# Start of a hybrid mLSTM / S5 / gated-FFN layer: S5 parameters loaded earlier and worked on between the statistics of x, the condition spread by PE transposes, the normalisation bias made on POOL

## The chip, the core and the metric

One core of one Trainium2 chip runs the kernel. The metric is the time of one execution on the device in microseconds (us); the kernel before has a median of 870.68 us over 3 runs (870.36 to 873.5).

## The reference, cut to what matters

One layer over x (512 tokens of 1024 features) with a condition vector c of 1024. Everything is float32.

```python
c_act = silu(c)
sh1, sc1, g1, sh2, sc2, g2 = split(c_act @ w_ada + b_ada, 6)
h   = standardize(x) * (1 + sc1) + sh1            # 512 x 1024
proj = h @ w_in + b_in                            # parts: mLSTM input, gates, S5 input, mixing gates
# S5 part, per state: dt = exp(log_dt); mag = exp(lam_re*dt); ar + i*ai = mag*(cos, sin)(lam_im*dt)
#   (zr, zi) from ar, ai, lam; powers of the rotation; a scan over the tokens
# mLSTM part: conv, q, k, v, chunked gated attention, norm, down projection
x = layer_norm(ALPHA * x + (1 + g1) * mix)        # then a gated FFN of 2816 and a second layer norm
```

## The kernel before, in words

**Layout.** Tokens lie in four tiles of 128 (`xt`), features in eight blocks of 128 (j or k = 0 to 7). A float32 product is made of three float32r matmuls (`mm3`, lines 255 to 258): high part by high part, high by low, low by high. So every operand is split first: ACT writes the high part (line 231) and DVE subtracts to get the low part (line 234).

**Start.** SP issues all loads from one queue, in program order: the small columns `cols`, the condition c broadcast over all 128 partitions (`CA`, 128 x 1024), the identity, the four x tiles, then the first weights (`wa1`, `w0`), then `lam`, the S5 parameters. ACT and DVE turn `CA` into c*(1+tanh(c/2)) in two halves (lines 308 to 311). A small copy `ca` (128 x 8, c with feature on partition) is made from `cols` at lines 312 to 316. For each x tile DVE takes statistics (`stats`: two of line 302, one of line 303), POOL makes the reciprocal deviation `rs` (lines 295, 296), DVE makes the bias `nb` = -mean*rs (line 329), and ACT normalises (line 324). While this runs, PE is kept busy with 34 matmuls on zeros (`warm`, line 338), and 9 more after the last transposes of the first block.

**Block steps k0 to k7 (`kstep`).** Step j needs scale and shift of feature block j: `ada1` (lines 343 to 348) multiplies two 128 x 1024 weight tiles by `CA` on DVE with a running sum, one per column of scale and shift. `htr(j)` transposes block j of the four normalised x tiles on PE (line 355), ACT applies scale and shift (line 357), and the result is split into `hp[j]`. Then PE runs 6 x 3 matmuls of 512 columns into six accumulators. Within step j the work for block j+1 is issued: its loads, `ada1(j+1)`, its weight split, and, after two of the six products, `htr(j+1)`.

**S5 parameters.** `s5_scalars` (lines 402 to 505) is a generator. Up to its first `yield` it works on DVE on 128 x 16 tiles: `exp_acc` (14 short instructions) for dt, a second `exp_acc` for mag, and polynomials for sine and cosine. The two stages after it are some 85 short POOL instructions (line 372 and its neighbours): `a1`, `zc` and the powers, then `epow` and the tables `e8`. `s5_params(q)` builds from them, for each of four groups q: `AB` (DVE, needs `zc` and the powers), its PE transposes into `G` (line 543), `TT`, `F` (DVE), and `E` (DVE, needs `e8`; line 208).

**What orders the work.** `SEQ` is an order written out by hand: each `S` advances the S5 generator to its next `yield`, each `H` the head generator (gates first, then four mLSTM heads), `u`, `x`, `o`, `g` are projection tiles. A planner then fills every engine's queue in that order of priority: an instruction of lower priority is put in where it reckons that the higher ones are not ready yet. `keep` fixes the order of some instructions of one engine, and `tc.issue_after(i)` puts a block's instructions behind instruction i on i's engine. At run time each engine works its queue in order, so an instruction that waits holds up all behind it on that engine.

The first gate work on PE are eight line 669 and four line 674 matmuls, then DVE computes the forget gates (lines 676 to 691), POOL lays them out (lines 698, 699) and PE transposes them (line 705).

Of the kernel before, what the change touches and what calls it, by code (L numbers as in the profile page):

```python
# [16 lines left out]
P = 128  # L17
# [37 lines left out]
def pack(i):  # L55
    f = np.float32
    a = {k: np.asarray(v) for k, v in i.items()}
    o = {}
    o["x"] = a["x"][0]
    wa = a["w_ada"][0].reshape(KD, P, 6, KD, P)  # L60
    o["wa1"] = wa[:, :, [1, 0]].transpose(3, 4, 2, 0, 1).reshape(KD, P, 2 * D)
    o["c"] = a["c"].reshape(1, D)
    o["wa2"] = wa[:, :, [4, 3, 2, 5]].reshape(KD, P, 4 * D)
    perm = np.arange(S).reshape(4, KD, C5).transpose(0, 2, 1).reshape(-1)
    w_in = a["w_in"][0]
    b_in = a["b_in"][0]
    o_i = 2 * D
    o_us = o_i + 8
    o_ga = o_us + S
    gg = np.arange(2 * D).reshape(2, KD, P).transpose(1, 0, 2).reshape(-1) + o_ga  # L70
    order = np.concatenate([o_us + perm, np.arange(o_i), gg])
    wt = w_in[:, order].reshape(KD, P, 36, P)
    bmain = b_in[order]
    o["w0"] = wt[:, :, :NXM0].reshape(KD, P, NXM0 * P)
    o["win"] = wt[:, :, NXM0:].transpose(2, 1, 0, 3).reshape(36 - NXM0, P, D)
    wg = np.zeros((KD, P, 32), f)
    wg[:, :, :8] = w_in[:, o_i:o_us].reshape(KD, P, 8)
    o["wg"] = wg.transpose(1, 0, 2).reshape(P, KD * 32)
    wq = a["w_mlstm_q"][0].reshape(2, 2, 2, P, QK)
    wk = a["w_mlstm_k"][0].reshape(2, 2, 2, P, QK)  # L80
    o["wqk"] = np.stack([wq, wk], 2).transpose(0, 4, 1, 2, 3, 5).reshape(2, P, D)
    o["wdn"] = a["w_mlstm_down"][0].reshape(KD, P, KD, P).transpose(2, 1, 0, 3).reshape(KD, P, D)
    o["wglu"] = a["w_s5_glu"][0][perm].reshape(4, P, 2, KD, P).transpose(3, 1, 2, 0, 4).reshape(KD, P, D)
    o["wmix"] = a["w_mix_out"][0].reshape(KD, P, D)
    o["wup"] = a["w_ffn_up"][0].reshape(KD, P, 2, NF, P).transpose(3, 2, 1, 0, 4).reshape(2 * NF, P, D)
    o["wfd"] = a["w_ffn_down"][0].reshape(NF, P, D)
    cols = np.zeros((P, NCOLS), f)

    def put(name, v):
        s, n = COLS[name]  # L90
        cols[:, s:s + n] = v

    ada = a["b_ada"][0].reshape(6, KD, P)
    put("c", a["c"][0].reshape(KD, P).T)
    put("ada1", ada[[1, 0]].transpose(2, 0, 1).reshape(P, 16))
    put("ada2", ada[[4, 3]].transpose(2, 0, 1).reshape(P, 16))
    put("b_in", bmain.reshape(36, P).T)
    put("b_gate", np.broadcast_to(b_in[o_i:o_us], (P, 8)))
    put("cw", a["w_mlstm_conv"][0].reshape(4, KD, P).transpose(2, 0, 1).reshape(P, 32))
    put("cb", a["b_mlstm_conv"][0].reshape(KD, P).T)  # L100
    put("gain", a["mlstm_norm_gain"][0].reshape(KD, P).T)
    put("d", a["s5_d"][0][perm].reshape(4, P).T)
    put("fw", a["w_ffn_conv"][0].reshape(3, NF, P).transpose(2, 0, 1).reshape(P, 66))
    put("fb", a["b_ffn_conv"][0].reshape(NF, P).T)
    o["rows"] = np.stack([ada[2].reshape(-1), ada[5].reshape(-1), a["ln1_gain"][0], a["ln1_bias"][0],
                          a["ln2_gain"][0], a["ln2_bias"][0]])
    lam = np.zeros((P, 3, NG), f)
    lam[:, 0] = a["s5_lam_re"][0].reshape(NG, P).T
    lam[:, 1] = a["s5_lam_im"][0].reshape(NG, P).T
    lam[:, 2] = np.repeat(a["s5_log_dt"][0].reshape(NG, 2).T, N5, 0)  # L110
    o["lam"] = lam.reshape(P, 3 * NG)
    bc = np.stack([np.stack([a["s5_b_re"][0], a["s5_b_im"][0]]),
                   np.stack([a["s5_c_re"][0], a["s5_c_im"][0]]).transpose(0, 1, 3, 2)])
    o["s5bc"] = bc.reshape(2, 2, 4, 4, P, C5).transpose(4, 2, 0, 1, 3, 5).reshape(P, 4, 256)
    o["ident"] = np.eye(P, dtype=f)
    mk = np.zeros((P, 16), f)
    mk[np.arange(16), np.arange(16)] = 1.0
    mk[32 + np.arange(16), np.arange(16)] = 1.0
    put("mask", mk)
    sg = np.zeros((P, 8), f)  # L120
    for j in range(8):
        sg[j::32, j] = 1.0
    put("selg", sg)
    o["cols"] = cols
    sh = np.zeros((P, T5, P), f)
    for t in range(T5):
        for s in range(t + 1):
            for q in range(C5):
                sh[(t - s) * C5 + q, t, (T5 - 1 - s) * C5 + q] = 1.0
    o["shift"] = sh.reshape(P, T5 * P)  # L130
    return {k: np.ascontiguousarray(v) for k, v in o.items()}
# [11 lines left out]
QUICK = (1, 3)  # L143
LAST = ((0, 0, 512), (1, 0, 256), (1, 256, 512))
SEQ = """
k0 S k1 S k2 k3 k4 S S S k5 k6 S S k7 H u0 x3 S S x2 S u1 u2 x1 S x0 H H o0 o3 S S S H H H H S S S H o1 S x5 H
H u3 H H H H S x6 o2 H H o4 H x7 S H H S H S H H H o6 S H H S x4 S S H H S o7 o5 H S H H S H g10 H H H H S g00
S S H S S S H H H S g20 H S H S S g01 H H H H H g30 H H H g11 S g31 S H H H H g21 A l0 A H H A g70 S l2 d0 S S
l1 d1 d2 g40 A g50 l3 A g41 A g51 S A A H H d3 l4 g60 R g61 A A A A A A l5 A A A d4 A A A l6 A A A d5 g71 l7
# [10 lines left out]
def _build(ctx, tc, nc, h):  # L160
# [9 lines left out]
    def const(shape, dt=F32):  # L170
        uid[0] += 1
        return sb.tile(list(shape), dt, name="k_%d" % uid[0])

    def bank(tag):
        return tl(tag, [P, 512], pool=ps)
# [7 lines left out]
    def hx(n=512, dt=F32, parts=P, tag="hx"):  # L183
        return tl(tag, [P, 516], dt)[:parts, :n]

    def hh(n=512, dt=F32, parts=P):
        return hx(n, dt, parts, "hh")
# [4 lines left out]
    def dma(o, i):  # L192
        return nc.sync.dma_start(o, i)  # L193

    def ts(o, i, a, b=None, op0=ALU.mult, op1=None):
        if op1 is None:
            V.tensor_scalar(o, i, a, None, op0=op0)
        else:
            V.tensor_scalar(o, i, a, b, op0=op0, op1=op1)

    def stt(o, i0, s, i1, op0=ALU.mult, op1=ALU.add, acc=None):
        if acc is None:
            V.scalar_tensor_tensor(o, i0, s, i1, op0=op0, op1=op1)  # L203
        else:
            V.scalar_tensor_tensor(o, i0, s, i1, op0=op0, op1=op1, accum_out=acc)

    def tt(o, a, b, op=ALU.mult):
        V.tensor_tensor(o, a, b, op=op)  # L208
# [14 lines left out]
    def keep(i):  # L223
        e = i.ins.engine
        if e in kept:
            tc.add_manual_dep(i.ins, kept[e].name, mybir.DependencyInfo(mybir.DependencyClass.NoSync, mybir.DependencyReason.DATA),
                              reason="order")
        kept[e] = i.ins

    def split_into(hi, lo, x, pin=False):  # L230
        i = A.copy(hi, x)  # L231
        if pin:
            keep(i)
        i = V.tensor_tensor(lo, x, f32(hi), op=ALU.subtract)  # L234
        if pin:
            keep(i)

    def wsplit(ap, n=D, tags=("wh", "wl"), w=None, pin=False):
        w = wload(ap, n) if w is None else w
# [21 lines left out]
    dma(cols, h["cols"])  # L261
    XB = const([P, 2, 4, 2, K5])
    CA = XB.rearrange("p r a g k -> p (r a g k)")
    dma(CA, h["c"].to_broadcast([P, D]))
    ident = const([P, P])
    dma(ident, h["ident"])
    xt = []
    for t in range(NT):
        xt.append(wload(h["x"][t * P:(t + 1) * P, :], tag="gab"))
# [6 lines left out]

    was = wa_load(0)
    w0 = w0_load(0)
    lam = const([P, 3, NG])
    dma(lam.rearrange("p a b -> p (a b)"), h["lam"])  # L280
    wgt = hx(256)
    dma(wgt, h["wg"])

# [21 lines left out]
        rstd_of(rs, mv[:, 1:2], 1)  # L305
        return mv[:, 0:1], rs

    for i, tw in enumerate((hx(), hh())):
        c_ = CA[:, i * 512:(i + 1) * 512]
        keep(A.activation(tw, c_, AF.Tanh, scale=0.5))  # L310
        stt(c_, tw, 1.0, c_, ALU.add, ALU.mult)
    th = const([P, 8])
    A.activation(th, col("c", 0, 8), AF.Tanh, scale=0.5)
    ca = const([P, 8])
    stt(ca, th, 1.0, col("c", 0, 8), ALU.add, ALU.mult)
    ts(ca, ca, 0.5)
    bhalf = const([P, 36])
    ts(bhalf, col("b_in", 0, 36), 0.5)
    norm = []
# [6 lines left out]
    for t, x in enumerate(xt):  # L326
        mu, rs = stats([x[:, :512], x[:, 512:]])
        nb = tl("nb", [P, 1], bufs=4)
        keep(V.scalar_tensor_tensor(nb, mu, -1.0, rs, op0=ALU.mult, op1=ALU.mult))
        norm.append((nb, rs))  # L330
        x_norm(t, 0, D if t < 2 else P)

# [10 lines left out]
    def ada1(j, wa):  # L343
        r = tl("adr", [P, 2], bufs=2)
        for i in range(2):
            keep(V.scalar_tensor_tensor(wa[i], wa[i], 0.5, CA, op0=ALU.mult, op1=ALU.mult, accum_out=r[:, i:i + 1]))
        keep(V.scalar_tensor_tensor(sc1[:, j:j + 1], r[:, 0:1], 1.0, col("ada1", j), op0=ALU.add, op1=ALU.add))
        keep(V.tensor_tensor(sh1[:, j:j + 1], r[:, 1:2], col("ada1", 8 + j), op=ALU.add))

# [52 lines left out]
    def s5_scalars():  # L402
# [23 lines left out]
        exp_acc(dt, lam[:, 2, :], NG)  # L426
        mag, ang = pt16(), pt16()
        tt(t16[0], lr, dt)
        exp_acc(mag, t16[0], NG)
        tt(ang, li, dt)  # L430
        kk = pt16()
        ts(kk, ang, 1.0 / (2 * math.pi), BIG, ALU.mult, ALU.add)
        ts(kk, kk, -BIG, None, ALU.add)
# [310 lines left out]
    acc0 = [acc() for _ in range(2)] + [bank("hd") for _ in range(4)]  # L744
    wbank = acc0[0]
    warm(wbank, 34)
    ada1(0, was)
    w0s = wsplit(None, NXM0 * P, w=w0, pin=True)
    lasttr = htr(0)
    with tc.issue_after(lasttr.ins):  # L750
        warm(wbank, 9)
    for t in (2, 3):
        x_norm(t, P, D)
    w0p = [w0s]
# [532 lines left out]
```

## Time and profile before

| | |
|---|---|
| median of 3 runs | 870.68 us |
| the profiled execution's own time | 870.72 us |
| its span, first to last instruction | 869.0 us |
| mean granted TensorE clock | 0.986 |
| PE busy | 831.4 us, 96% |
| DVE busy | 625.2 us, 72% |
| ACT busy | 366.9 us, 42% |
| POOL busy | 106.3 us, 12% |

The span is the time on the cores' engines; the execution's own time has 1.7 us more around it. A busy time counts instructions in work, not how well they use the engine; matmuls on zeros count as busy too. "Idle before <-" in a row is the time for which the engine stood still before that instruction and what ended the wait. The granted clock is given as a share of full speed (1.00 is 2.4 GHz, 0.50 is 1.2 GHz).

### The profile page before, as it was taken

How to read it: one execution, taken by the hardware profiler on the slowest of the kernel's cores; microseconds unless marked ns; L12 is line 12 of the kernel's file. 1: busy time of each engine (PE TensorE's matmuls, PEld its weight loads, DVE VectorE, ACT ScalarE, POOL GpSimd, SP SyncE). 2: the span in 40 equal slices, each digit the busy share in tenths (PEclk: the TensorE clock that was granted, in tenths of full speed). 3: DMA queues.
4: the chain of work that ended last, by engine and by line, in shares of the span. 5: the costliest groups of instructions: out<-in, count | busy, mean ns of one | idle time of the engine just before them, and what ended most of it. 6: DMA issues, size and time to landing. Idle time of an engine off the chain costs nothing.

```text
span 869.0 us, 11151 instructions
## 1 busy us (share of the span) xinstructions
PE 831.4 (96%) x4005; PEld 669.6 (77%) x4005; DVE 625.2 (72%) x1169; ACT 366.9 (42%) x585; POOL 106.3 (12%) x256
## 2 busy tenths in 40 slices
PE   6979999999999999999999999999999999999996
PEld 2756778787778778888887988888888878888885
DVE  5967888978779785558988858566666675878144
ACT  3445445553565533223334456444444444334000
POOL 2298121112022000000002200000000000000000
PEclk8889999999999999999999999999999999999999
DMA  8742231222222243558656013224344232445011
GB/s 318 256 150 89 67 106 37 83 70 85 66 63 65 72 137 129 186 186 285 227 172 216 14 49 121 97 93 139 135 142 146 98 121 73 157 160 172 22 49 48
DMA packets 45558, 106.45 MB, mean 122 GB/s; under 512 B 13376, under 2 KB 14272, under 8 KB 45504
## 3 DMA queue, kind: packets, MB, share of 16 engines
q1 hardware_dynamic: 45504, 105.75, 36.8%
q8 instruction: 31, 0.51, 0.2%
q14 instruction: 23, 0.19, 0.1%
HBM read 101.54 MB, written 2.10 MB: 119 GB/s over the span
## 4 chain that ended last, share of the span: by engine, by line
PE 68%; DVE 15%; POOL 6%; ACT 4%; DMA 3%; issue 2%; SPq 2%; DVEq 0%; ACTq 0%; POOLq 0%
PE acc L258 10%; PE acc L257 10%; PE hd L256 10%; PE acc L256 10%; PE hd L258 10%; PE hd L257 10%; POOL k L372 3%; DVE hh L203 2%; DVE wl L234 2%; SPq L193 2%; DVE s5h L208 2%; PE s L256 1%; PE s L257 1%; PE s L258 1%; PE s L636 1%
## 5 line engine op out<-in xcount | busy, mean ns | idle before, releaser
L231 ACT CAST wh<-w 128x1024 fp32r<-128x1024 f32 (+2 forms) x103 | 103.1, 1003 | 143.4 <-PE acc L257 107.4
L234 DVE TENSOR_TENSOR wl<-w,wh 128x1024 fp32r<-128x1024 f32 (+2 forms) x103 | 120.9, 1175 | 57.8 <-ACT wh L231 56.0
L256 PE MATMUL acc<-hp,wh 128*128 128x512 f32 x256 | 103.0, 407 | 4.8 <-ACT hp L231 4.2
L257 PE MATMUL acc<-hp,wh 128*128 128x512 f32 x256 | 102.0, 399 | 0.3 <-DVE hp L234 0.3
L258 PE MATMUL acc<-hp,wl 128*128 128x512 f32 x256 | 101.8, 398 | 0.0
L256 PE MATMUL hd<-s5b,wh 128*128 128x512 f32 (+1 forms) x168 | 63.2, 379 | 0.7 <-ACT s5b L1199 0.5
L257 PE MATMUL hd<-s5b,wh 128*128 128x512 f32 (+1 forms) x168 | 63.7, 380 | 0.1
L258 PE MATMUL hd<-s5b,wl 128*128 128x512 f32 (+1 forms) x168 | 63.5, 379 | 0.0
L256 PEld LDWEIGHTS acc<-hp,wh 128*128 128x128 f32 x256 | 48.7, 192 | 18.3 <-ACT hp L231 6.3
L203 DVE SCALAR_TENSOR_TENSOR hh<-hh,hh 128x512 f32<-128x512 f32 x52 | 36.0, 692 | 31.2 <-ACT hh L591 14.7
L257 PEld LDWEIGHTS acc<-hp,wh 128*128 128x128 f32 x256 | 48.9, 191 | 10.1 <-DVE hp L234 1.0
L258 PEld LDWEIGHTS acc<-hp,wl 128*128 128x128 f32 x256 | 48.9, 191 | 9.8
L203 DVE SCALAR_TENSOR_TENSOR s5h<-hh,k,s5h 128x512 f32<-128x512 f32 x56 | 39.3, 747 | 3.3 <-DMA hh<-in_wa 3.0
L1054 POOL TENSOR_SCALAR mov<-mov 128x1 f32<-128x1 f32 x6 | 4.3, 724 | 274.5 <-ACT s L1053 158.5
L256 PEld LDWEIGHTS hd<-s5b,wh 128*128 128x128 f32 x168 | 31.3, 188 | 7.6 <-ACT s5b L1199 0.8
L257 PEld LDWEIGHTS hd<-s5b,wh 128*128 128x128 f32 x168 | 31.6, 188 | 7.2 <-DVE s5b L234 0.6
L258 PEld LDWEIGHTS hd<-s5b,wl 128*128 128x128 f32 x168 | 31.6, 188 | 6.4
L203 DVE SCALAR_TENSOR_TENSOR hh<-hh,k,hh 128x512 f32<-128x512 f32 x44 | 33.0, 751 | 4.5 <-ACT hh L1216 3.6
L257 PE MATMUL acc<-hx,wh 128*128 128x512 f32 x84 | 33.2, 395 | 0.0
L258 PE MATMUL acc<-hx,wl 128*128 128x512 f32 x84 | 33.1, 394 | 0.0
L256 PE MATMUL acc<-hx,wh 128*128 128x512 f32 x84 | 33.0, 393 | 0.0
L258 PE MATMUL acc<-s5b,wl 128*128 128x512 f32 x80 | 31.7, 397 | 0.5 <-DVE wl L234 0.5
(552 smaller groups left out, 2079.3 us busy)
## 6 DMA issues: line engine op xcount, KB each, us to landing
w<-in_wup SPq DMA_DIRECT2D x44, 512.0 KB, 3.3
hh<-in_wa SPq DMA_DIRECT2D x64, 256.0 KB, 3.9
w<-in_win SPq DMA_DIRECT2D x30, 512.0 KB, 3.3
w<-in_wfd SPq DMA_DIRECT2D x22, 512.0 KB, 3.3
hb<-in_wa SPq DMA_DIRECT2D x16, 512.0 KB, 7.2
w<-in_wglu SPq DMA_DIRECT2D x8, 512.0 KB, 3.3
w<-in_wdn SPq DMA_DIRECT2D x8, 512.0 KB, 3.5
w<-in_wmix SPq DMA_DIRECT2D x8, 512.0 KB, 4.0
```

The costliest lines, as they stand in the source:

```text
L193: return nc.sync.dma_start(o, i)
L203: V.scalar_tensor_tensor(o, i0, s, i1, op0=op0, op1=op1)
L208: V.tensor_tensor(o, a, b, op=op)
L231: i = A.copy(hi, x)
L234: i = V.tensor_tensor(lo, x, f32(hi), op=ALU.subtract)
L256: T.matmul(o, lhsT=wh, rhs=xh, start=first, stop=False)
L257: T.matmul(o, lhsT=wh, rhs=xl, start=False, stop=False)
L258: T.matmul(o, lhsT=wl, rhs=xh, start=False, stop=last)
L372: GP.tensor_tensor(o, a, b, op=op)
L636: T.matmul(o, lhsT=F[:, ri, pr, :], rhs=XB[:, ri, pr].rearrange("p g k -> p (g k)"), start=ri == 0, stop=False)
L1054: GP.tensor_scalar(v[:, 2:3], v[:, 0:1], v[:, 1:2], EPS * D, op0=ALU.add, op1=ALU.add)
```

## The change

- `c` is no longer loaded broadcast. `ca` (now made first) is copied over 128 columns per block on DVE, eight PE transposes against the identity turn that into rows of c in two PSUM banks (tag `s5`), and ACT copies the banks into `CA`. `ca` holds the factor 0.5 already, so `ada1` multiplies by 1.0.
- `lam` is the third load, ahead of the x tiles.
- `nb` is made on POOL (one tensor_scalar with two pointer scalars), behind `rs` on the same engine; it is no longer in DVE's kept order.
- `s5_scalars` has one more `yield`: after dt (and the two products with it). The generator is advanced to it right behind the 34 warm matmuls, ahead of `ada1(0)`, and advanced through the rest of the DVE part behind the low split of `hp[0]` on DVE.
- `SEQ` places the following steps anew: `a1`, `zc` and powers after k0, `epow` and `e8` after k1, `AB` after k5, `G` after k6, `TT` and `F` after k7. `E` and all later steps stand where they stood against the projection tiles.
- 12 instead of 9 warm matmuls stand behind the last transpose of the first block.

```diff
--- before.py
+++ after.py
@@ -59,7 +59,6 @@
     o["x"] = a["x"][0]
     wa = a["w_ada"][0].reshape(KD, P, 6, KD, P)
     o["wa1"] = wa[:, :, [1, 0]].transpose(3, 4, 2, 0, 1).reshape(KD, P, 2 * D)
-    o["c"] = a["c"].reshape(1, D)
     o["wa2"] = wa[:, :, [4, 3, 2, 5]].reshape(KD, P, 4 * D)
     perm = np.arange(S).reshape(4, KD, C5).transpose(0, 2, 1).reshape(-1)
     w_in = a["w_in"][0]
@@ -143,7 +142,7 @@
 QUICK = (1, 3)
 LAST = ((0, 0, 512), (1, 0, 256), (1, 256, 512))
 SEQ = """
-k0 S k1 S k2 k3 k4 S S S k5 k6 S S k7 H u0 x3 S S x2 S u1 u2 x1 S x0 H H o0 o3 S S S H H H H S S S H o1 S x5 H
+k0 S k1 S k2 k3 k4 k5 S k6 S k7 S S H u0 x3 S S x2 S u1 u2 x1 S x0 H H o0 o3 S S S H H H H S S S H o1 S x5 H
 H u3 H H H H S x6 o2 H H o4 H x7 S H H S H S H H H o6 S H H S x4 S S H H S o7 o5 H S H H S H g10 H H H H S g00
 S S H S S S H H H S g20 H S H S S g01 H H H H H g30 H H H g11 S g31 S H H H H g21 A l0 A H H A g70 S l2 d0 S S
 l1 d1 d2 g40 A g50 l3 A g41 A g51 S A A H H d3 l4 g60 R g61 A A A A A A l5 A A A d4 A A A l6 A A A d5 g71 l7
@@ -234,6 +233,9 @@
         i = V.tensor_tensor(lo, x, f32(hi), op=ALU.subtract)
         if pin:
             keep(i)
+            last_lo[0] = i.ins
+
+    last_lo = [None]
 
     def wsplit(ap, n=D, tags=("wh", "wl"), w=None, pin=False):
         w = wload(ap, n) if w is None else w
@@ -261,9 +263,10 @@
     dma(cols, h["cols"])
     XB = const([P, 2, 4, 2, K5])
     CA = XB.rearrange("p r a g k -> p (r a g k)")
-    dma(CA, h["c"].to_broadcast([P, D]))
     ident = const([P, P])
     dma(ident, h["ident"])
+    lam = const([P, 3, NG])
+    dma(lam.rearrange("p a b -> p (a b)"), h["lam"])
     xt = []
     for t in range(NT):
         xt.append(wload(h["x"][t * P:(t + 1) * P, :], tag="gab"))
@@ -276,8 +279,6 @@
 
     was = wa_load(0)
     w0 = w0_load(0)
-    lam = const([P, 3, NG])
-    dma(lam.rearrange("p a b -> p (a b)"), h["lam"])
     wgt = hx(256)
     dma(wgt, h["wg"])
 
@@ -305,15 +306,17 @@
         rstd_of(rs, mv[:, 1:2], 1)
         return mv[:, 0:1], rs
 
-    for i, tw in enumerate((hx(), hh())):
-        c_ = CA[:, i * 512:(i + 1) * 512]
-        keep(A.activation(tw, c_, AF.Tanh, scale=0.5))
-        stt(c_, tw, 1.0, c_, ALU.add, ALU.mult)
     th = const([P, 8])
     A.activation(th, col("c", 0, 8), AF.Tanh, scale=0.5)
     ca = const([P, 8])
     stt(ca, th, 1.0, col("c", 0, 8), ALU.add, ALU.mult)
     ts(ca, ca, 0.5)
+    V.tensor_copy(CA.rearrange("p (a b) -> p a b", a=8), ca[:, :, None].to_broadcast([P, 8, P]))
+    cb_ = [bank("s5"), bank("s5")]
+    for i in range(8):
+        T.transpose(cb_[i // 4][:, (i % 4) * P:(i % 4 + 1) * P], CA[:, i * P:(i + 1) * P], ident)
+    for i in range(2):
+        keep(A.copy(CA[:, i * 512:(i + 1) * 512], cb_[i]))
     bhalf = const([P, 36])
     ts(bhalf, col("b_in", 0, 36), 0.5)
     norm = []
@@ -326,7 +329,7 @@
     for t, x in enumerate(xt):
         mu, rs = stats([x[:, :512], x[:, 512:]])
         nb = tl("nb", [P, 1], bufs=4)
-        keep(V.scalar_tensor_tensor(nb, mu, -1.0, rs, op0=ALU.mult, op1=ALU.mult))
+        GP.tensor_scalar(nb, mu, rs, -1.0, op0=ALU.mult, op1=ALU.mult)
         norm.append((nb, rs))
         x_norm(t, 0, D if t < 2 else P)
 
@@ -343,7 +346,7 @@
     def ada1(j, wa):
         r = tl("adr", [P, 2], bufs=2)
         for i in range(2):
-            keep(V.scalar_tensor_tensor(wa[i], wa[i], 0.5, CA, op0=ALU.mult, op1=ALU.mult, accum_out=r[:, i:i + 1]))
+            keep(V.scalar_tensor_tensor(wa[i], wa[i], 1.0, CA, op0=ALU.mult, op1=ALU.mult, accum_out=r[:, i:i + 1]))
         keep(V.scalar_tensor_tensor(sc1[:, j:j + 1], r[:, 0:1], 1.0, col("ada1", j), op0=ALU.add, op1=ALU.add))
         keep(V.tensor_tensor(sh1[:, j:j + 1], r[:, 1:2], col("ada1", 8 + j), op=ALU.add))
 
@@ -426,8 +429,9 @@
         exp_acc(dt, lam[:, 2, :], NG)
         mag, ang = pt16(), pt16()
         tt(t16[0], lr, dt)
+        tt(ang, li, dt)
+        yield
         exp_acc(mag, t16[0], NG)
-        tt(ang, li, dt)
         kk = pt16()
         ts(kk, ang, 1.0 / (2 * math.pi), BIG, ALU.mult, ALU.add)
         ts(kk, kk, -BIG, None, ALU.add)
@@ -744,11 +748,14 @@
     acc0 = [acc() for _ in range(2)] + [bank("hd") for _ in range(4)]
     wbank = acc0[0]
     warm(wbank, 34)
+    next(side)
     ada1(0, was)
     w0s = wsplit(None, NXM0 * P, w=w0, pin=True)
     lasttr = htr(0)
     with tc.issue_after(lasttr.ins):
-        warm(wbank, 9)
+        warm(wbank, 12)
+    with tc.issue_after(last_lo[0]):
+        next(side)
     for t in (2, 3):
         x_norm(t, P, D)
     w0p = [w0s]
```

## Rows read from the trace of the kernel before

**Rows 1.** The page: busy time of each engine, its share of the span, instructions.

```profile
PE 831.4 (96%) x4005; PEld 669.6 (77%) x4005; DVE 625.2 (72%) x1169; ACT 366.9 (42%) x585; POOL 106.3 (12%) x256
```

**Rows 2.** Busy time by stretch: stretch (start:end) and its length in us, busy us and count of PE, PEld, DVE, ACT and POOL, then granted clock, DMA share, GB/s.

```profile
5.70:11.00 5.30, 5.30 (x25) 2.21 (x23) 2.42 (x6) 1.32 (x3) 0.80 (x2) 1.00 1.02 412
22.30:26.00 3.70, 3.40 (x9) 2.30 (x9) 3.63 (x12) 2.72 (x3) 0.00 (x0) 0.50 0.70 201
47.10:50.00 2.90, 2.88 (x7) 2.30 (x8) 2.90 (x4) 1.65 (x2) 2.90 (x4) 0.50 0.76 242
60.00:64.20 4.20, 4.09 (x33) 3.17 (x33) 0.09 (x1) 2.69 (x5) 3.71 (x17) 0.59 0.34 125
...
22.30:92.70 70.40, 59.57 (x283) 45.76 (x283) 56.30 (x176) 30.17 (x42) 44.45 (x106) 0.92 0.50 162
22.60:69.60 47.00, 39.61 (x180) 30.63 (x180) 39.27 (x121) 20.05 (x29) 29.50 (x62) 0.89 0.58 189
39.90:81.00 41.10, 32.74 (x169) 24.81 (x168) 28.78 (x59) 19.01 (x28) 38.70 (x89) 0.92 0.46 150
45.60:59.90 14.30, 9.79 (x36) 7.67 (x36) 13.57 (x28) 5.22 (x7) 13.59 (x23) 0.88 0.43 141
59.90:64.10 4.20, 4.02 (x32) 3.19 (x32) 0.00 (x0) 2.59 (x5) 3.71 (x18) 0.59 0.34 125
...
22.30:840.00 817.70, 795.47 (x3844) 646.20 (x3845) 599.62 (x1109) 357.13 (x570) 97.64 (x225) 0.99 0.37 120
```

**Rows 3.** DMA issues of the start: destination <- source, KB of one, median us from issue to landing; then, from the chain of waits, issue and flight of the first x tile (start us, us).

```profile
k<-in_c SPq DMA_DIRECT2D x1, 512.0 KB, 4.8
...
2.17 5.89 DMA gab<-in_x
```

**Rows 4.** DVE in order of time, the start: start us, us, line, operation, out<-in, and the idle time before it in brackets.

```profile
3.37 0.17 DVE L197 TENSOR_SCALAR k<-k 128x8 f32<-128x8 f32 x1
8.09 1.29 DVE L302 BATCH_NORM_STATS2 st<-gab 128x6 f32<-128x512 f32 x2 [4.55 <-DMA gab<-in_x]
9.41 0.21 DVE L303 BATCH_NORM_AGGREGATE mv<-st 128x2 f32<-128x12 f32 x1
16.65 0.16 DVE L329 SCALAR_TENSOR_TENSOR nb<-mv,rs 128x1 f32<-128x1 f32 x1 [1.00 <-POOL rs L296]
16.73 0.69 DVE L203 SCALAR_TENSOR_TENSOR k<-hx,k 128x512 f32<-128x512 f32 x1
17.34 0.73 DVE L203 SCALAR_TENSOR_TENSOR k<-hh,k 128x512 f32<-128x512 f32 x1
18.13 1.21 DVE L346 SCALAR_TENSOR_TENSOR hb<-hb,k 128x1024 f32<-128x1024 f32 x1
20.57 0.15 DVE L348 TENSOR_TENSOR k<-adr,k 128x1 f32<-128x1 f32 x1
22.64 0.69 DVE L234 TENSOR_TENSOR hp<-hx,hp 128x512 fp32r<-128x512 f32 x1
```

**Rows 5.** ACT and PE in order of time, the start.

```profile
16.85 0.49 ACT L324 ACTIVATE gab<-gab,nb,rs 128x128 f32<-128x128 f32 x1 [1.51 <-DVE nb L329]
17.66 4.05 PE L338 MATMUL acc<-k 128*128 128x512 bf16 x9
20.81 0.78 ACT L357 ACTIVATE hx<-s,k,k 128x512 f32<-128x512 f32 x1 [2.75 <-DVE k L348]
21.62 0.62 ACT L231 CAST hp<-hx 128x512 fp32r<-128x512 f32 x1
22.29 0.80 PE L256 MATMUL acc<-hp,wh 128*128 128x512 f32 x1 [0.58 <-ACT hp L231]
```

**Rows 6.** The S5 parameters: last instruction for dt on DVE, last one of the DVE part, and the first of the POOL chain that follows.

```profile
28.39 0.17 DVE L203 SCALAR_TENSOR_TENSOR k<-ea,eai 128x16 f32<-128x16 f32 x1
39.65 0.16 DVE L199 TENSOR_SCALAR k<-k 128x16 f32<-128x16 f32 x1
39.89 0.63 POOL L372 TENSOR_TENSOR k<-k,k 128x32 f32<-128x32 f32 x1 [0.47 <-DVE k L199]
```

**Rows 7.** One group of POOL instructions of that chain in two stretches: from 45.6 to 59.9 us, and from 59.9 to 64.1 us: count | busy us, mean ns of one | idle before.

```profile
L372 POOL TENSOR_TENSOR k<-k,k 128x32 f32<-128x32 f32 x13 | 8.6, 664 | 0.6
L372 POOL TENSOR_TENSOR k<-k,k 128x32 f32<-128x32 f32 (+1 forms) x10 | 2.5, 260 | 0.2
```

**Rows 8.** The waits of PE and DVE between 40 and 95 us, in order of time.

```profile
45.15 0.32 DVE L208 TENSOR_TENSOR s5h<-s5h,k 128x128 f32<-128x128 f32 x1 [2.33 <-POOL k L372]
47.12 1.22 PE L256 MATMUL acc<-hp,wh 128*128 128x512 f32 x2 [3.20 <-ACT hp L231]
59.97 1.70 PE L543 MATMUL s<-k,s5b 128*128 128x128 f32 x8 [3.06 <-DVE s5b L208]
64.11 0.70 DVE L234 TENSOR_TENSOR hp<-hx,hp 128x512 fp32r<-128x512 f32 x1 [4.29 <-ACT hp L231]
81.07 0.43 DVE L208 TENSOR_TENSOR s5h<-k,k 128x256 f32<-128x256 f32 x1 [2.90 <-POOL k L372]
92.75 2.16 PE L705 MATMUL hd<-k,hh 128*16 128x128 f32 x12 [1.93 <-POOL hh L698]
```

**Rows 9.** Prices for added operations: POOL's tensor_scalar at line 295 in order of time, and that of line 1054 as a group (count | busy us, mean ns of one | idle before).

```profile
9.71 0.23 POOL L295 TENSOR_SCALAR rs<-mv 128x1 f32<-128x1 f32 x1 [7.80 <-DVE mv L303]
L1054 POOL TENSOR_SCALAR mov<-mov 128x1 f32<-128x1 f32 x6 | 4.3, 724 | 274.5 <-ACT s L1053 158.5
```

## The prediction

> **What bounds the kernel now.** I read the page first: PE is busy 96% of the span [rows 1], so an engine that becomes faster is worth only what PE stops losing. Busy time by stretch then says where PE loses. Between 22.3 and 840 us it is busy 795.47 of 817.70; between 22.3 and 92.7 alone it is busy 59.57 of 70.40 [rows 2], so about half of its 22 us of standing lies in the block steps and just behind them, and everything ahead of 22.3 is start. Last come the engines in order of time, to see who releases whom. The first real matmul stands at 22.29, released by ACT's split, which waited for DVE's shift column at 20.57 [rows 4, 5]. PE then loses 3.20 us before 47.12 and 3.06 before 59.97 [rows 8], and each time the granted clock falls: 0.50 (1.2 GHz) from 47.1 to 50.0, 0.59 from 60.0 to 64.2, as at the start from 22.3 to 26.0 [rows 2]. Both waits are DVE's. At 45.15 it stood 2.33 us for the POOL chain with the shift column queued behind; at 59.97 PE's transposes for G waited for AB while the next block's transposes stood behind them, which is also why DVE stood 4.29 before 64.11 [rows 8]. At 81.07 DVE waits 2.90 for the chain's end (E), and the gates behind it reach PE at 92.75, 1.93 late [rows 8]. So three things count: when PE starts, whether the block steps stall, and when POOL's chain ends.
>
> **The start.** x keeps its place as fourth issue on SP's queue, so it is not issued earlier; c goes and lam takes its slot. What falls away is c's 512 KB [rows 3], at the 412 GB/s of that stretch [rows 2] 1.27 us. Between nothing and this I take it whole, since the queues are full there: first statistics at 6.8 instead of 8.09.
>
> From there DVE took 12.6 us to the shift column (8.09 to 20.72). Four biases go (4 x 0.16), with their waits for POOL (1.00 the last; the one read for the first tile was 0.45, and I take the other two the same: 2.35 in all; the first three rest on my reading of DVE's order, of which the last is shown), and the two products on CA (0.69 + 0.73): 4.4 us [rows 4]. Added are the 16 instructions for dt. Each is busy 0.17 [rows 6], so 2.7 us in line, nothing if all fall into waits; I take 1.5, since a tile's statistics (1.29 + 0.21, rows 4) last longer than its 1.27 us of transfer and leave few waits. Shift column: 6.8 + 12.6 - 4.4 + 1.5 = 16.5, 4.2 earlier; low split of block 0 at 18.4 instead of 22.64.
>
> POOL's bias costs 0.23 to 0.72 a tile [rows 9], where DVE's cost 0.16 and a hop; I take 0.5, off DVE's path and on that of the last tile only. The c path (a DVE copy of 128 x 1024, at most the 1.21 of the product of that size; eight transposes, 1.70 as those for G; two ACT passes of 0.62; rows 4, 5, 8) starts at 3.5, when `ca` is done, and ends near 8, ahead of ada1: nothing, covered by DVE's wait for x. If the planner put the transposes behind all warm matmuls, on which PE was busy to the end of the stretch up to 11.0 [rows 2], it would end near 14, still ahead of ada1(0). The third load costs SP no more than c's slot did.
>
> PE need not follow by 4.2. The last tile's norm ends near 16 (16.85 + 0.49 before, rows 5), and 12 warm matmuls at 0.45 (4.05 / 9, rows 5) last until 21.4 at 1.2 GHz, half as long at 2.4. First real matmul: 18.1 to 21.4, I take 19.8, 2.5 earlier, and of the 1.85 us that half clock cost from 22.3 to 26.0 [rows 2] I give back 1. Start: 3.5 at PE, 4.2 at DVE.
>
> **The block steps.** The 41 short instructions behind dt ran from 28.56 to 39.81 among the block work, 11.3 us [rows 6]. They now begin behind the low split at 18.4 and at the same pace end at 29.8: POOL starts 10 us earlier. AB goes one step later, to a time (about 45) when `zc` (5.3 us after POOL's start before) has long been there, so the 2.33 and with it the 3.20 go. G's transposes go behind k6, when the next block's are already done: the 3.06 goes, and DVE's 4.29 shrinks to about 1. With the slow clock behind both (0.50 x 2.9 and 0.41 x 4.2, rows 2: 1.45 + 1.7), PE would reach the gates 3.5 + 3.2 + 3.1 + 3.15, some 13 us earlier.
>
> **What is late next** is E, with the gates behind it. POOL's chain has 89 instructions between 39.9 and 81.0 [rows 2]. Beside a busy DVE (13.57 of 14.3 us) 23 of them took 14.3 us, 0.62 each; with DVE idle 18 took 4.2, 0.23 each [rows 2]; one form alone took 664 and 260 ns [rows 7]. The Trainium skill, GPSIMD Engine Reference, section 8 (Key points), says that GpSimd shares its SBUF interfaces with VectorE and contends with DVE instructions that have two SBUF inputs; these rows agree. DVE ran out of its own work at 78.2 (81.07 less 2.90); less 4.2 (start), 1.4 (about half of dt's sixteen, at 0.17, lay behind 22.6, since the last stands at 28.39, rows 6), 2.33 and 3.3 (waits gone) it does so at 67. From 29.9 to 67 POOL does 37 / 0.62 = 60, the other 29 at 0.23 take 6.8: 73.8, E near 74.1. That is 7.0 earlier than 81.07. From E to PE's line 705 nothing changes (11.7 us), so PE is 7 earlier there, though it could have been 13. Behind 92.7 PE stands only 11 of 747 us [rows 2] and its work is the same, so I carry the 7 to the end.
>
> **Sum.** 870.72 (span 869.0 and 1.7 around it) - 7.0 = 863.7, taken as 863.5; the profiled execution lies 0.04 over the median, so no correction.
>
> **Rivals.** (a) *Gates ahead of E.* If the planner puts the gates' DVE work before E, or POOL meets more idle time of DVE, E no longer holds PE and all 13 remain: 857.5. For it: DVE's work from 22.6 to 69.6 was 39.27 of 47.0 us [rows 2], so it has room. Against: before, E stood ahead. (b) *POOL no earlier than the start.* The short instructions now rank ahead of block 1, but each needs the one before, and long ones slip in between; if that stretches their 11.3 to 17 us, POOL starts 4 us earlier only and, by the rates above, E comes some 3 earlier: 867.8. Here too: the change does not do what it says, dt lies among the weight products and not between statistics, and DVE gains little at the start. (c) *Slower: POOL starved.* With stalls gone DVE works without a pause and two-input instructions fill it; if all 89 take 0.62, the chain ends at 29.9 + 55.2 = 85.1, E is 4.4 late and the gates hold PE: 875.1. It decides from 0.57 us an instruction (51.1 / 89); before the mean was 0.46 (41.1 / 89). By the skill's rule on two-input instructions, held to throughout, this is the case that follows. Against it: DVE's own work ends before E.
>
> **How the numbers follow.** A measurement of this kernel tells about 0.5% (4.4 us) from no change. Forecast 0.55 (860 to 866.2), (a) 0.17, (b) 0.20, (c) 0.08. Faster by over 0.5% (below 866.3): forecast, (a) and a little of (b), 0.75; same 0.17; slower 0.08. The range 857 to 868.5 holds the forecast, about half of (a) and most of (b). The unknown costs lie in it: dt at 0 to 2.7, x at 0 to 1.27, bias at 0.23 to 0.72, first matmul 18.1 to 21.4.
>
> **What would show it.** First statistics near 6.8; no DVE wait for `rs`; shift column near 16.5; the first POOL instruction of the chain near 30; no PE wait over 1 us before the end of k7, granted clock 1.00 from about 23; POOL's mean near 0.5 between; E near 74 with DVE waiting longer than 2.90; line 705 near 86. A chain that ends later than 81, or a new PE wait in k1 (the short instructions ahead of ada1(1)), would make me wrong.

## The result, and the profile after

The changed kernel takes 883.76 us (median of 4 runs, 881.72 to 886.44) against 871.26 (4 runs): a ratio of 1.0141, 95% interval 1.0105 to 1.0178. The forecast was 863.5. The change made the kernel 12.5 us slower. The profiled execution took 886.44 us, the longest of the four, with a span of 884.7 and a mean granted clock of 0.975 (0.986 before).

The waits of PE over the whole span, by line waited for: total us, times, longest. One wait stands out, and it has no counterpart in [rows 8]; line 554 is the first matmul of `kt`, the first step towards `TT`. It reads `cb`, a copy of `ct` (part of the S5 group's load) spread out between zeros. Four POOL instructions make `cb`: they turn the sign of half of `ct`, write the zeros and copy two halves.

```profile
PE s L554 <- POOL s5h L542: 11.5, 1, 11.5
PE s L358 <- ACT gab L327: 3.6, 3, 2.0
PE s L640 <- DVE k L210: 3.0, 2, 1.6
PE acc L258 <- ACT hp L230: 2.5, 2, 1.8
```

Busy time by stretch, columns as in [rows 2]:

```profile
22.40:62.40 40.00, 37.50 (x173) 28.71 (x171) 34.60 (x93) 19.58 (x27) 31.90 (x56) 1.00 0.66 217
62.40:73.80 11.40, 0.00 (x0) 0.00 (x0) 1.54 (x2) 2.28 (x3) 10.54 (x37) 0.64 0.19 66
73.80:79.00 5.20, 5.17 (x28) 1.65 (x31) 1.52 (x2) 2.06 (x4) 1.17 (x6) 0.50 0.00 0
...
137.50:143.50 6.00, 6.00 (x18) 4.46 (x19) 5.63 (x16) 3.66 (x9) 1.53 (x4) 0.50 0.26 89
297.00:308.00 11.00, 10.87 (x43) 9.19 (x43) 7.28 (x14) 4.37 (x9) 1.21 (x3) 0.53 0.13 48
29.60:72.60 43.00, 30.30 (x138) 22.77 (x136) 29.56 (x57) 19.73 (x26) 40.47 (x86) 0.92 0.53 175
30.00:59.90 29.90, 27.44 (x126) 20.75 (x125) 27.51 (x55) 14.65 (x21) 28.13 (x43) 1.00 0.64 209
60.40:72.60 12.20, 1.96 (x9) 1.30 (x7) 1.24 (x1) 4.28 (x5) 11.47 (x44) 0.71 0.28 89
```

The block steps are what I had hoped for: from 22.4 to 62.4 PE is busy 37.50 of 40.0 us at full clock. Then from 62.4 to 73.8 it does nothing, with DVE busy 1.54 us of it and ACT 2.28; only POOL works throughout (10.54). After that PE runs 5.2 us at 0.50 (1.2 GHz).

The queues in order of time show why. POOL had written the zeros at the start (1.75 us), but it comes to the other three instructions for `cb` only when its chain is done (first row below). DVE's `F` waits for the first of those three (the sign of `ct`, line 370), PE's line 554 for the last (line 542). Line 709 is PE's transposes of the gates, line 705 in [rows 8], where they stood at 92.75.

```profile
72.16 0.46 POOL L375 TENSOR_TENSOR k<-k,hh 128x128 f32<-128x128 f32 x1
72.58 0.40 POOL L370 TENSOR_SCALAR s5h<-s5h 128x64 f32<-128x64 f32 x1
73.04 0.41 POOL L541 COPY s5h<-s5h 64x128 f32<-64x128 f32 x1
73.48 0.29 POOL L542 COPY s5h<-s5h 64x128 f32<-64x128 f32 x1
...
73.01 0.29 DVE L207 TENSOR_TENSOR s5h<-s5h,k 128x128 f32<-128x128 f32 x1 [8.55 <-POOL s5h L370]
...
61.97 0.39 PE L260 MATMUL hd<-hp,wl 128*128 128x512 f32 x1
73.83 1.08 PE L554 MATMUL s<-s5b,s5h 128*32 128x128 f32 x16 [11.47 <-POOL s5h L542]
...
94.66 0.54 PE L709 MATMUL hd<-k,hh 128*16 128x128 f32 x2 [0.62 <-POOL hh L702]
96.25 2.36 PE L709 MATMUL hd<-k,hh 128*16 128x128 f32 x10 [1.05 <-POOL hh L702]
```

In the kernel before, the same three instructions lay in the middle of the chain. Its POOL queue, in order of time, and then PE's last matmul of the block steps:

```profile
46.76 0.40 POOL L367 TENSOR_SCALAR s5h<-s5h 128x64 f32<-128x64 f32 x1
47.85 1.28 POOL L537 COPY s5h<-s5h 64x128 f32<-64x128 f32 x1
50.71 0.97 POOL L538 COPY s5h<-s5h 64x128 f32<-64x128 f32 x1
...
74.91 0.39 PE L258 MATMUL hd<-hp,wl 128*128 128x512 f32 x1
```

Counted in the trace, they are POOL's instructions 46, 48 and 51 there and 119 to 121 after the change, behind every instruction of the tables `e8`. (The expectations below give places one or two higher.)

So PE reached the end of the block steps some 13 us earlier (its last matmul of them starts at 61.97, before at 74.91), and gave back 11.5 in one wait, 2.6 on the half clock behind it, and more later: the gates' transposes begin 1.9 us later than before and end 3.7 us later, and the span ends 15.7 later. Behind the gates this execution has two more stretches at half clock, 6 us and 11 us long (above), worth about half of their length, 8 us; the kernel before shows none there.

### The profile page after: what moved, and what is told of

It is laid out like the page before. It is cut to its first block, busy times and chain, and to the rows that moved or that the text cites. A ratio compares the mean times of both kernels' runs of the same rounds, so it can differ in the third digit from the quotient of the medians.

```text
span 884.7 us, 11166 instructions
## 1 busy us (share of the span) xinstructions
PE 840.3 (95%) x4015; PEld 675.3 (76%) x4016; DVE 621.1 (70%) x1164; ACT 367.9 (42%) x585; POOL 120.5 (14%) x260
## 4 chain that ended last, share of the span: by engine, by line
PE 65%; DVE 15%; POOL 7%; ACT 5%; issue 3%; DMA 3%; SPq 1%; DVEq 0%; ACTq 0%; POOLq 0%
PE hd L258 10%; PE acc L258 9%; PE hd L259 9%; PE acc L260 9%; PE acc L259 9%; PE hd L260 9%; POOL k L375 4%; DVE hh L202 3%; DVE s5h L207 2%; DVE s5b L207 2%; DVE wl L233 2%; PE s L258 1%; PE s L259 1%; PE s L260 1%; PE s L640 1%
## 5 line engine op out<-in xcount | busy, mean ns | idle before, releaser
L1220 POOL MEMSET hh<- 128x2 f32 x22 | 2.2, 100 | 227.4 <-DVE hh L202 107.0
```

What stands on the lines that cost most here:

```text
L1220: GP.memset(gb_[:, 0:2], 0.0)
```

## The experiments

Each run was timed against the kernel before on the same chip; that has a median of 871.3 to 871.9 in these comparisons. Ratios are to it. The first group asks whether the place of `cb` in POOL's queue is the loss (theory Q) or the later order of the new plan (theory T). Every `SEQ` line is cut behind `u0`.

**cb_dve.** The changed kernel, `cb` of the first group on DVE:

```diff
-        gts(ct[:, 1], ct[:, 1], -1.0)
-        GP.memset(cb, 0.0)
-        GP.tensor_copy(cb[0:64, :, :, 0:C5], ct[0:64])
-        GP.tensor_copy(cb[64:P, :, :, C5:32], ct[64:P])
+        X = V if q == 0 else GP
+        X.tensor_scalar(ct[:, 1], ct[:, 1], -1.0, None, op0=ALU.mult)
+        X.memset(cb, 0.0)
+        X.tensor_copy(cb[0:64, :, :, 0:C5], ct[0:64])
+        X.tensor_copy(cb[64:P, :, :, C5:32], ct[64:P])
```

> The changed kernel with one edit: the four short POOL instructions that prepare cb for the first S5 group (sign of ct, zeros, two copies) run on DVE. Theory Q (POOL's queue: in the changed kernel these instructions stand behind the whole chain for e8, and PE stood 11.5 us for them, DVE 8.6): the wait of 11.5 goes, the gates' transposes (line 709 there, 96.2 us) come near 84 to 87, and the time is 862 to 868 us. Theory T (the later order of the new plan costs some 11 us by itself, behind the gates): the wait goes but the time stays at 872 to 876.

Measured: 872.07 us (10 runs, 865.36 to 875.07), ratio 1.0005 (0.9983 to 1.0028). The wait is gone and 11.7 us with it. The gates' transposes come at 82.89, and DVE's work for the gates (line 681) now stands ahead of E (line 207, the last row):

```profile
82.89 1.96 PE L710 MATMUL hd<-k,hh 128*16 128x128 f32 x12 [2.71 <-POOL hh L703]
68.41 0.19 DVE L681 TENSOR_TENSOR k<-hd,k 128x32 f32<-128x32 f32 x1 [1.45 <-PE hd L679]
76.57 0.41 DVE L207 TENSOR_TENSOR s5h<-k,k 128x256 f32<-128x256 f32 x1
```

That is 9.9 earlier than before, and earlier than the 84 to 87 of theory Q. But the time is T's, not Q's. This profile is of the fastest of the ten runs (865.36), and 4 us of the 9.9 are lost again behind the gates; in a second profile (cb_dve_look, 872.71) it is nearly 10. Both theories hold a part.

**start_only.** The start as changed; the extra `yield`, the early advances and the new `SEQ` taken back:

```diff
-k0 S k1 S k2 k3 k4 k5 S k6 S k7 S S H u0
+k0 S k1 S k2 k3 k4 S S S k5 k6 S S k7 H u0
...
-    next(side)
     ada1(0, was)
...
-    with tc.issue_after(last_lo[0]):
-        next(side)
```

> The start alone: c spread by PE transposes, lam third, bias on POOL, 12 warm matmuls; S5 steps, their order and the place of dt as in the kernel before. The plan puts cb's instructions at the end of POOL's chain here too, with G and kt on PE ahead of k6 and k7. Theory Q: PE waits for cb from about 57 until the chain ends near 78, some 15 to 20 us, and the time is 883 to 892. Theory T: only the start's gain shows, 866 to 868.

**start_only_cb** is the same with the edit of cb_dve.

> The start alone as in start_only, with cb of the first group on DVE. Theory Q: no wait for cb; the start's 3 to 4 us are left, perhaps with a shorter POOL chain: 864 to 868. Theory T: the same, 866 to 868; what tells the two apart is its distance to start_only (15 us or more by Q, nothing by T).

Measured: start_only 875.87 us (6 runs), ratio 1.0042 (1.0018 to 1.0066); start_only_cb 861.71 us (4 runs), ratio 0.9894 (0.9866 to 0.9922). The pair differs by 14.2 us; start_only_cb is faster than either theory had it. Even without any S5 step moved, start_only stands for `cb`, line 553 there:

```profile
53.30 1.94 PE L546 MATMUL s<-k,s5b 128*128 128x128 f32 x8 [2.11 <-DVE s5b L207]
70.69 1.08 PE L553 MATMUL s<-s5b,s5h 128*32 128x128 f32 x16 [13.80 <-POOL s5h L541]
84.23 1.92 PE L672 MATMUL hd<-hx,hx 128*32 128x512 f32 x16 [0.80 <-ACT hx L802]
```

Its time was under Q's range by 7. The wait was 13.8 and not 15 to 20, as the chain ended near 70; that is 1 to 6 of the 7.

**lam_only.** The kernel before with one load moved, from eleventh to fourth place:

```diff
     dma(ident, h["ident"])
+    lam = const([P, 3, NG])
+    dma(lam.rearrange("p a b -> p (a b)"), h["lam"])
...
     w0 = w0_load(0)
-    lam = const([P, 3, NG])
-    dma(lam.rearrange("p a b -> p (a b)"), h["lam"])
```

> The kernel before with one edit: lam is the fourth load, ahead of x, instead of the eleventh. In its plan cb's POOL instructions stand behind the chain for e8 instead of in its middle; PE's order is that of before. Theory Q (the place in POOL's queue is the cost): PE waits 14 to 18 us for cb at line 550, the clock falls, 880 to 888 us. Theory T (the loss came from other parts of the change): a load of 24 KB moved forward changes nothing, 870 to 872.

Measured: 880.70 us (4 runs), ratio 1.0094 (1.0061 to 1.0127). This is the sharpest run: no computation was moved in the program, yet the kernel is 9 us slower, by the same wait. The wait is shorter than the 14 to 18 expected; the time lies in Q's range.

```profile
73.43 1.08 PE L550 MATMUL s<-s5b,s5h 128*32 128x128 f32 x16 [11.74 <-POOL s5h L538]
```

With lam's load earlier, the planner puts `cb` at places 115 to 117 of POOL's queue instead of 46 to 51. Why its reckoning turns over there I read from the queues only (it would have the chain done sooner, and `cb` later); that is argued, not shown.

**cb_early.** The changed kernel, `cb` on POOL but ahead of the chain (places 30 to 32). `cb_make` holds the four lines of `cb`, which `s5_params` then leaves out for the first group; both are cut here:

```diff
+    dma(bc0[:, :256], h["s5bc"][:, 0, :])
+    cb_make(bc0)
     for t in (2, 3):
         x_norm(t, P, D)
```

> The changed kernel with cb of the first group left on POOL, but its load issued behind wg and its four instructions made ahead of the chain (place 32 to 34 in POOL's queue instead of 120 to 122). Theory Q: the wait of 11.5 goes as in cb_dve, 866 to 873. If instead the work had to leave POOL: 880 to 885.

Measured: 872.38 us (10 runs), ratio 1.0004 (0.9978 to 1.0030), the same as cb_dve. So POOL may do this work; only its place matters.

**before_cb.** The kernel before with the edit of cb_dve.

> The kernel before with cb of the first group on DVE. The POOL chain loses three instructions that took 2.65 us in its middle, so E comes 2 to 3 us earlier: 867.5 to 869.5 if E is what holds the gates, 870 to 872 if not. By theory Q the edit helps only this much here, since cb did not stand behind the chain; if it gave 8 us or more here too, the gain of the two pairs would be DVE's doing and not that of the queue's order.

Measured: 869.34 us (7 runs), ratio 0.9970 (0.9950 to 0.9991). Moving the work to DVE is worth 2.5 us by itself, against 11.7 and 14.2 where it also takes `cb` out from behind the chain.

**seq_old_cb.** cb_dve with the S5 steps at their old places:

```diff
-k0 S k1 S k2 k3 k4 k5 S k6 S k7 S S H u0
+k0 S k1 S k2 k3 k4 S S k5 k6 S S k7 H u0
```

> The changed kernel with the S5 steps at their places of before (AB and G behind k4, TT and F behind k6) and cb of the first group on DVE. Theory Q: no wait for cb; chain early, so 860 to 866; a wait for AB ahead of G, as before (3 us), may come back. Theory T: as the later order is nearly that of before again, 861 to 866; cb_dve stays above it by 8 or more by T, by less than 4 by Q.

Measured: 861.93 us (4 runs), ratio 0.9901 (0.9881 to 0.9921), 10.1 below cb_dve. Q's bound of 4 is missed: the new places of the steps are a loss of their own. It equals start_only_cb (861.71), so doing the DVE part early bought nothing that shows. The loss is not all clock: the fastest runs of cb_dve and start_only_cb have the same mean clock, 0.996, and lie 6.5 us apart (865.36 and 858.87).

On the path through E this kernel does what the prediction had worked out. E stands ahead of the gates and waits for the chain's end, and the gates' transposes follow 11.7 us behind it:

```profile
74.73 0.42 DVE L207 TENSOR_TENSOR s5h<-k,k 128x256 f32<-128x256 f32 x1 [2.22 <-POOL k L375]
86.41 1.95 PE L710 MATMUL hd<-k,hh 128*16 128x128 f32 x12 [1.12 <-POOL hh L703]
```

**seq_tf_late and seq_ag_late** split that loss: both are cb_dve with one half of the places taken back.

```diff
 seq_tf_late
+k0 S k1 S k2 k3 k4 S S k5 k6 k7 S S H u0
 seq_ag_late
+k0 S k1 S k2 k3 k4 k5 S k6 S S S k7 H u0
```

> The changed kernel with cb of the first group on DVE, AB and G back behind k4, TT and F left behind k7. Theory F (TT and F behind k7 put the first group's S5 run later among the projections and heads, and the waits and clock falls that this leaves are the 10 us between cb_dve and seq_old_cb): 868 to 874. Theory G (AB and G behind k5 and k6 are the cost): 860 to 864.

> The changed kernel with cb of the first group on DVE, AB behind k5 and G behind k6 as in the change, TT and F ahead of k7 as before. From the gates on PE's planned order is that of seq_old_cb. Theory F: 858 to 863. Theory G: 868 to 874.

Measured: seq_tf_late 869.95 us (10 runs), ratio 0.9984 (0.9970 to 0.9998); seq_ag_late 864.41 us (6 runs), ratio 0.9926 (0.9903 to 0.9949). Theory F: `TT` and `F` behind k7 cost 8.0 against seq_old_cb; `AB` and `G` late cost 2.5, with intervals that overlap (and seq_ag_late lies 1.4 above F's range). What the 8 are made of is less clear. PE's waits between 84 and 440 us sum to 13.5 in seq_tf_late and 9.8 in seq_old_cb, 3.7 more. The two profiled runs have the same mean clock, 0.990, and lie 5.0 apart (869.34 and 864.36); so in this pair the clock is not the main part, and what the waits leave over stays open.

**cb_dve_look** is cb_dve once more, for a second profile.

> cb_dve once more, for another profile: its ten runs lay between 865 and 875 with a mean clock of 0.996 to 0.981. If falls of the clock behind waits of 1 to 3 us make the spread, a run near 872 shows one or more stretches at 0.50 behind such waits after 80 us, and its matmul order and waits are those of the first profile. If the waits themselves are longer, the profile shows those.

Measured: 872.71 us, with a span 7.4 us longer than in the first profile. The same stretches, first of the run with 865.36, then of this one, each with the longest wait ahead of its last stretch:

```profile
8.00:16.00 8.00, 5.17 (x27) 2.55 (x26) 6.60 (x21) 4.29 (x7) 5.66 (x11) 1.00 1.01 384
16.00:24.00 8.00, 8.00 (x32) 4.74 (x31) 7.09 (x36) 5.57 (x8) 0.00 (x0) 0.79 0.97 362
124.00:132.00 8.00, 7.53 (x64) 6.39 (x63) 6.98 (x24) 4.69 (x13) 1.29 (x4) 1.00 0.18 64
284.00:296.00 12.00, 12.00 (x84) 11.04 (x84) 9.01 (x31) 4.51 (x12) 2.13 (x4) 1.00 0.31 84
...
279.85 0.50 PE L258 MATMUL hd<-hb,hb 128*128 128x512 f32 x1 [1.31 <-ACT hb L874]
```

```profile
8.00:16.00 8.00, 5.23 (x25) 2.29 (x23) 7.42 (x25) 3.41 (x5) 5.91 (x12) 0.97 1.02 382
16.00:24.00 8.00, 7.12 (x21) 3.79 (x23) 6.27 (x26) 5.29 (x7) 0.08 (x1) 0.60 0.97 344
124.00:132.00 8.00, 7.17 (x24) 5.62 (x25) 7.63 (x20) 4.89 (x11) 2.01 (x6) 0.57 0.18 67
284.00:296.00 12.00, 11.87 (x47) 9.80 (x47) 7.82 (x15) 4.37 (x9) 1.19 (x3) 0.57 0.12 44
...
283.92 0.50 PE L258 MATMUL hd<-hb,hb 128*128 128x512 f32 x1 [1.31 <-ACT hb L874]
```

In the second one the clock is 0.57 to 0.60 in three stretches, in the first it falls only at the start. The waits ahead of the later two are those of the first profile (1.59 and 1.60 ahead of the first of them, 1.31 in both rows above; 13.3 us in sum from 84 to 440, against 12.3). The same short waits are followed by a fall of the clock in one run and not in another.

**nb_only and c_only_cb** take the start apart. nb_only is the kernel before with the bias on POOL; c_only_cb is before_cb with c spread by PE transposes (no edit shown).

```diff
 nb_only
-        keep(V.scalar_tensor_tensor(nb, mu, -1.0, rs, op0=ALU.mult, op1=ALU.mult))
+        GP.tensor_scalar(nb, mu, rs, -1.0, op0=ALU.mult, op1=ALU.mult)
```

> The kernel before with the normalisation bias made on POOL, nothing else. DVE loses four short instructions and their waits for rs, 2.9 us of the start; cb stays in the middle of POOL's chain. Theory Q: 868 to 870. Theory T: no change, 870 to 872.

> The kernel before with cb of the first group on DVE and c spread by PE transposes; lam and the bias as before, 9 warm matmuls. Against before_cb (869.3) it lacks c's 512 KB ahead of x (1.3 us) and two DVE products (1.4 us): 866 to 867.5. If c is what gave most of the 8 us between before_cb and start_only_cb: 862 to 864; if lam's place and the chain's earlier start did: 867 to 869.

Measured: nb_only 870.56 us (10 runs), ratio 0.9976 (0.9964 to 0.9988): 1.3 us, less than Q said, and its time lies in T's range. c_only_cb 865.79 us (6 runs), ratio 0.9937 (0.9914 to 0.9959), 3.6 below before_cb, with intervals that just overlap. With `cb` out of the way the start as a whole is worth some 7 us (869.34 to 861.71).

seq_old_cb and start_only_cb beat both kernels, by 9.4 to 9.6 us against the one before.

## Why the prediction was wrong

**The failed step** is the wait of PE that the prediction put at nothing. I priced POOL's chain for one reader only ("What is late next is E"), and took the order of POOL's queue as it was, without a reason. The step of G issues the four POOL instructions for `cb` too, and in "The block steps" I moved G by its PE transposes alone ("G's transposes go behind k6"), though `kt` on PE and `F` on DVE read from the same queue. With `cb` behind the chain, the chain's end holds PE directly. That is 11.5 us and the half clock behind it; cb_dve and start_only_cb, beside their kernels with `cb` left in its place, and cb_early show that it is the queue's order. G's new place is not needed for it: in start_only and lam_only G stands where it stood, and lam's earlier load alone turns the order over. Whether G's new place alone would do so too, no run shows.

**A second step** failed with it: I took the new places of `TT` and `F` as free and carried the gain at the gates to the end ("its work is the same"). seq_tf_late says 8 us. With `cb` on DVE and `TT` and `F` at their old places, the path through E was right: in seq_old_cb E begins at 74.73 (74.1 worked out), and the transposes stand at 86.41 (near 86). That its time, 861.93, is so near 863.5 is in part luck: PE still waits 3.99 us for `AB` there, and the move of `cb` to DVE is worth 2.5 by itself.

**My slower rival** (c) named the right engine and the wrong mechanism: POOL was not starved. The chain ended at 72.6, ahead of the 73.8 that I worked out; in cb_dve, where DVE did not stand beside it for 8.55 us, it ended at 73.75.

Point by point, what the prediction said would show it:

- First statistics near 6.8: they stand at 5.91, 2.2 us earlier than before, where that term was bounded at 1.27. No DVE wait for `rs`: right. Shift column near 16.5: it is done at 14.67.

```profile
5.91 1.29 DVE L303 BATCH_NORM_STATS2 st<-gab 128x6 f32<-128x512 f32 x2 [0.46 <-DMA gab<-in_x]
4.68 0.69 DVE L314 COPY k<-k 128x1024 f32<-128x1024 f32 x1
14.51 0.16 DVE L351 TENSOR_TENSOR k<-adr,k 128x1 f32<-128x1 f32 x1
13.48 1.41 POOL L297 TENSOR_TENSOR rs<-rs,k 128x1 f32<-128x1 f32 x1
14.99 0.27 POOL L332 TENSOR_SCALAR nb<-mv,rs 128x1 f32<-128x1 f32 x1
17.21 0.62 ACT L230 CAST hp<-hx 128x512 fp32r<-128x512 f32 x1
16.96 4.43 PE L341 MATMUL acc<-k 128*128 128x512 bf16 x10 [0.22 <-issue]
21.37 0.71 PE L258 MATMUL acc<-hp,wh 128*128 128x512 f32 x2
```

- First real matmul at 19.8: 21.37, inside the bounds (18.1 to 21.4) and at their late end. DVE was done 6.1 us sooner than before, but one instruction of the last tile's `rs` on POOL took 1.41 us beside the weight products, and its bias began at 14.99. The high part of block 0 was ready at 17.83, but the 12 warm matmuls ran until 21.4 at half clock. By these rows they held the first real one for some 3.5 us; no run took them out.
- POOL's chain from 30: its first instruction stands at 29.62. Block steps without a PE wait over 1 us: one of 1.79 at 57.03, else right, with the clock at 1.00.
- POOL's mean near 0.5: 86 instructions in 43.0 us. Beside a busy DVE they took 0.70 (43 in 29.9), beside an idle one 0.28 (44 in 12.2); the prediction had 0.62 and 0.23. The contention that [rows 7] show was sized nearly right.
- E near 74, line 705 near 86: E began at 89.7 behind `F` and the gates, and the transposes stood at 94.66 and 96.25. In cb_dve, with the one wait gone, E began at 76.57 and the transposes at 82.89: the gates stood ahead of E, which is rival (a), but its time did not follow, since the gain was lost behind the gates.

Most terms of the sum were thus near; an edge between queues was missing from it.

## What to carry to other kernels

When a step is moved, list what it puts into every queue, the helpers on the slow engine above all, and ask what stands ahead of each in that queue: two readers on PE and DVE waited 11.5 and 8.6 us for three POOL instructions of 1.1 us. Where a planner fills the queues, even an earlier load can turn their order over (lam_only: 9 us), so compare each queue's order before and after, not only the times. Put short instructions that a busy engine waits for ahead of a long chain, or on another engine.

## What the runs showed of the hardware that was not expected

Half clock is not a fixed price of a wait: with the same program and nearly the same waits of 1 to 3 us, one profiled run of it took 865.36 us at a mean clock of 0.996 (cb_dve) and another 872.71 at 0.983 (cb_dve_look). A DVE copy of 128 x 1024 float32 took 0.69 us, where the two-input product of that size takes 1.21 [rows 4].
